# An encoder layer on one core: the order of VectorE and ScalarE at the start of the second FFN is written by hand for one block more

## The chip, the cores and the metric

One core of a Trainium2 chip runs the whole layer. The metric is the device time of one execution in microseconds (us). The engines are named as in the profile: PE (TensorE), DVE (VectorE), ACT (ScalarE), POOL (GpSimd), SP (the engine whose queue issues the DMAs).

## The reference

One post-norm encoder layer on 1024 tokens of width 1024, in float32: a first half-step FFN, attention beside a state-space scan, a second half-step FFN, and a gated embedding, each followed by a layer norm. The change lies in the second FFN:

```
gate, up = split(x @ w_in)            # w_in: 1024 x 5632, so 2816 gate and 2816 up columns
x = LN2(alpha*x + 0.5*((silu(gate) * up) @ w_out))
```

## The kernel before

**Tiling.** The 2816 hidden columns are 22 blocks of 128, called block 0 to block 21 here. For one block, gate and up together are a product of a 1024 x 256 weight with the activations of 1024 x 1024, done as a 2 x 2 product of quadrants by a Strassen-Winograd scheme with 7 products. Two of them use the gate weights as they are (quadrants B11 and B21 of the activations; `ffn_first`, L280); the other five use sums of weight quadrants and the activation operands T2, T1, T3, T4 and B22, in this order (`ffn_rest`, L367 to 392). Each of the seven is four contraction steps of 128, and each step is three matmuls, because every float32 operand is kept as a rounded high part and a low part (hi x lo, lo x hi, hi x hi; `mm3`, L115). So one product is 12 matmuls of 128 x 512.

**What surrounds a product.** A high part is a copy on ACT (`split` L108, `put_later` L247), the low part a subtraction on DVE (`lo`, L87). A product's result lies in one of four PSUM tiles `sm`; it is read out by DVE or ACT, and only then may a later product write into that tile. In `ffn_rest`: T2's is read by the sum `u2` (L378, DVE), T1's by the copy `p5` (L381, ACT), T3's by `u3` (L384, DVE), T4's by a second sum onto `u3` (L387, DVE), B22's by the sum into `sg` (L388, DVE). After it come Silu (L389, ACT), two multiplications (L390 and 391, DVE) and the stores of `h` with their sums (`left_factors`, L339 to 363). The weight sums s1 to s4 are L267 to 270, on DVE for blocks 1 to 6 and on POOL later.

**The beginning.** Blocks 0 to 4 have their first two products made early, while the activations are still being normalised. The activation operands are made for the second half of the tokens by `Sums` (L1708 to 1735): `one` to `four` are subtractions (L1705), followed by a high part on ACT and a low part on DVE; `last` makes the high and low parts of B22 (tiles `xh` and `xl`). `in_turn` issues these so that the low part of one follows the step of the next. Blocks 0 and 1 take their weights from the ring of `blk` tiles; from block 2 on the weights come through the four tiles `raw`, whose memory is that of the eight tiles `acc1`, so the first load of `raw` waits for the last reader of those: the low parts of B22. Two loads (gate and up) serve one block.

**What sets the order.** PE executes in the order of the code (`in_order(PE)` around the whole kernel). From L1779 to L1851 DVE and ACT do too (`with self.in_order(Activation, DVE)`): instructions traced in that stretch keep their order on the engine. Everything else is placed by a scheduler, which may also set instructions of its own between those of the stretch. In the kernel before, the stretch ends with `later(*sums[2:])` for block 1; the five products of block 0 (`ffn_rest` for block 0) lie behind it and the scheduler places what reads them. For blocks 2, 3 and 4 the sum of the two early products (`first_sum`, L290) is a function that `ffn_h` calls when it reaches the block; the scheduler places it.

The names in the rows: `xET2`, `xET1`, `xET3` with h or l are T2, T1, T3; in this stretch `xl<-acc` written after `xET3` is first T4 and then B22.

Of the kernel before, what the change touches and what calls it, by code (L numbers as in the profile page):

```python
# [9 lines left out]
F32 = mybir.dt.float32  # L10
F32R = mybir.dt.float32r
BF16 = mybir.dt.bfloat16
AF = mybir.ActivationFunctionType
ALU = mybir.AluOpType
# [4 lines left out]
P = 128  # L19
S = 1024  # L20
D = 1024
NT = S // P
# [14 lines left out]
class Layer:  # L37
# [332 lines left out]
    def ffn_rest(self, X, tmp, to, blocks, p1, sg, between=(), G=None):  # L370


        between = list(between)
        nc = self.nc
        V, G, A = nc.vector, G or nc.gpsimd, nc.scalar
        b2, b1, b3, b22, b4 = blocks
        u2, u3, p5 = (tmp.tile([P, 512], F32, name=name) for name in ("u2", "u3", "p5"))
        V.tensor_tensor(out=u2, in0=p1, in1=self.product(b2, X["T2"]), op=ALU.add)  # L378
        if between:
            between.pop(0)()  # L380
        A.copy(out=p5, in_=self.product(b1, X["T1"]))  # L381
        if between:
            between.pop(0)()
        V.tensor_tensor(out=u3, in0=u2, in1=self.product(b3, X["T3"]), op=ALU.add)  # L384
        G.tensor_tensor(out=u2, in0=u2, in1=p5, op=ALU.add)
        G.tensor_tensor(out=p5, in0=u3, in1=p5, op=ALU.add)
        V.tensor_tensor(out=u3, in0=u3, in1=self.product(b22, X["T4"]), op=ALU.add)  # L387
        V.tensor_tensor(out=sg[:, 512:], in0=u2, in1=self.product(b4, X["B22"]), op=ALU.add)  # L388
        A.activation(out=sg, in_=sg, func=AF.Silu)  # L389
        V.tensor_tensor(out=sg[:, :512], in0=sg[:, :512], in1=u3, op=ALU.mult)  # L390
        V.tensor_tensor(out=sg[:, 512:], in0=sg[:, 512:], in1=p5, op=ALU.mult)
        to(sg)

    def ffn_h(self, X, wi, tmp, store, pre=(), done=0, aside=None, raws=(), mixed=None, upto=0):

        nc = self.nc

        def first(f):
            g, u = raws if f == done and raws else (self.raw(wi[f, 0]), self.raw(wi[f, 1]))
            p1, sg = (pre[f]() if callable(pre[f]) else pre[f]) if f < len(pre) else self.ffn_first(X, tmp, tmp.tile([P, S], F32, name="sg"), g)
            return (g, u, tmp), p1, sg

        prev = None
        for f in range(done, NF + 1):
            s = first(f) if f < NF else None
            self.pop(2)
            if prev:  # L410
                left = mixed if f == done + 1 and mixed else self.mixed_sums(*prev[0], nc.vector if f <= upto + 1 else nc.gpsimd)

                self.ffn_rest(X, tmp, lambda h: store(f - 1, h), [b() if callable(b) else self.split(b) for b in left], *prev[1:], G=nc.vector if f == NF or f <= upto + 1 else None)
            for _ in range(0 if f < 4 or not aside else 2 if f % 4 == 0 and f > 4 else 1):
                aside.pop(0)()
            prev = s
# [1106 lines left out]
    def run(self):  # L1523
        nc, tc, I = self.nc, self.tc, self.I
# [7 lines left out]
        with ExitStack() as c:  # L1532
            pool = c.enter_context(tc.tile_pool(name="xE", bufs=1))
            tmp = self.ffn_work(c, 0)
            tmp.more()
            tmp.all()
            hS, store = self.left_factors(0, tmp)
            wpool, wT, steps = self.right_sums(c, 0, I["wo1"])
            with self.in_order(mybir.EngineType.Activation, mybir.EngineType.DVE):
                X, pre, blocks0, raws1, blocks1 = self.begin(pool, tmp, wpool)  # L1540
# [20 lines left out]
        with ExitStack() as c:  # L1561
# [4 lines left out]
            blocks0, aside = [], []  # L1566
# [112 lines left out]
        with ExitStack() as xc:  # L1679
            pool = xc.enter_context(tc.tile_pool(name="xE", bufs=1))  # L1680
            X = {n: [pool.tile([P, 4, 512], F32R, name=f"xE{n}{j}") for j in "hl"] for n in ("T1", "T2", "T3")}
            X["B11"], X["B21"], X["B22"] = self.unit(0, 0), self.unit(0, 1), self.unit(1, 0)
            V = nc.vector
            tmp = self.ffn_work(xc, 1)
            tmp.more()

            def w(i, j, to=None):
                r = self.ring.tile([P, 1024], F32, name="blk") if to is None else to
                nc.sync.dma_start(out=r, in_=I["wi2"][i, j])
                return r  # L1690
# [9 lines left out]
            def plain(t):  # L1700
                for do in [put(name, t, acc[t + i].rearrange("p (k t) -> p k t", k=4), 2) for i, name in enumerate(("B11", "B21"))]:
                    do()
# [32 lines left out]
            def in_turn(steps):  # L1735

                waiting = None
                for step in steps:
                    do = step()
                    if waiting:  # L1740
                        waiting()
                    waiting = do
                waiting()

            def gate(g):
                return zip(*[self.split_later(g[:, m]) for m in (lo, hi)])

            def later(*dos):
                for do in dos:
                    do()  # L1750
# [8 lines left out]
            blocks0 = {}  # L1759
            pre = []  # L1760
            X["T4"] = self.unit(1, 1)
            def left_block(i):
                blocks0[i], do = self.split_later(left[i])
                return do

            with self.in_order(mybir.EngineType.Activation, mybir.EngineType.DVE):
                left, sums = self.mixed_steps(g0, u0, tmp, V)
                later(*sums[:2])
                plain(0)
                later(*sums[2:])  # L1770
                plain(2)
                r5, r6, r7 = (Row(t) for t in (5, 6, 7))
                r5.half(0)
                r5.half(1)
                r5.root()
                r5.factors()
                r5.shift()

                r6.half(0)  # L1779
                r7.half(0)  # L1780
                w0, lo0 = gate(g0)
                w1, lo1 = gate(sgs[1])
                later(*lo0)
                r6.half(1)
                r6.root()
                flip(4)
                later(*lo1)
                r6.factors()
                r6.shift()
                r7.half(1)  # L1790
                r7.root()
                w2, lo2 = gate(sgs[2])
                lo_s2 = left_block(0)
                lo_a22 = left_block(3)
                s = {t: Sums(t, tmp.tile([P, 512], F32, name=n)) for t, n in ((4, "u3"), (5, "u2"))}
                s[4].one()
                t14 = s[4].put1()
                r7.factors()
                r7.shift()
                s[4].two()  # L1800
                t24 = s[4].put2()
                s[5].one()
                t15 = s[5].put1()
                s[5].two()
                t25 = s[5].put2()
                p0 = first(w0)
                later(lo_a22, t14, t15)
                pre.append(self.first_kept(sgs[0], p0))
                w3, lo3 = gate(sgs[3])
                lo_s1 = left_block(1)  # L1810
                later(*lo2, t24, t25, lo_s2)
                p1 = first(w1, lambda: flip(6))
                later(*lo3, lo_s1)
                s.update({t: Sums(t, tmp.tile([P, 512], F32, name=n)) for t, n in ((6, "h3"), (7, "p5"))})
                s[6].one()
                s[6].two()
                self.first_copy(sgs[1], p1)
                w4, lo4 = gate(sgs[4])
                t26 = s[6].put2()
                s[7].one()  # L1820
                s[7].two()
                t27 = s[7].put2()
                t26()
                t16 = s[6].put1()
                t27()
                t17 = s[7].put1()
                pre.append(self.first_sum(sgs[1], p1))

                def both(f, p):
                    for q, m in zip(p, (hi, lo)):  # L1830
                        nc.scalar.copy(out=sgs[f][:, m], in_=q)
                    pre.append(lambda: self.first_sum(sgs[f], [None, sgs[f][:, lo]]))
                both(2, first(w2))
                later(t16, t17, *lo4)
                p3 = first(w3)
                in_turn([s[t].three for t in range(4, NT)])
                both(3, p3)
                lo_s3 = left_block(2)
                both(4, first(w4))
                lo_s3()  # L1840
                in_turn([s[t].four for t in range(4, NT)])
                left_block(4)()
                g1, u1 = w(1, 0), w(1, 1)
                left, sums = self.mixed_steps(g1, u1, tmp, V)
                later(*sums[:2])
                in_turn([s[t].last for t in range(4, NT)])
                b2 = self.split(left[0])
                later(*sums[2:])
            blocks0 = [blocks0[i] for i in range(5)]
            hS, store = self.left_factors(1, tmp)  # L1850
            self.ffn_rest(X, tmp, lambda h: store(0, h), blocks0, *pre[0], G=V)  # L1851
            actx.close()
            self.open_raw(rctx, 4)
            tmp.all()
# [103 lines left out]
```

## Time and profile before

| | us |
|---|---|
| median of 3 runs | 1958.57 (1957.98 to 1959.1) |
| the profiled execution | 1959.67 |
| its span, first to last instruction | 1957.8 |
| PE busy in the span | 1931.1 (99%) |
| PE waiting in the beginning of the second FFN | 3.81 in one piece |

The profiled execution is one run on its own, 1.10 us above the median, and 1.87 us of it lie outside the span. The times in the rows count from the span's start. A row of the timeline is an instruction or a run of equal ones: start, duration, engine, line, operation, out<-in. What stands in brackets is the time for which the engine stood idle before it, and what ended the idle time.

### The profile page before, as it was taken

The page shows a single profiled execution, that of the slowest core. Times are in us where ns is not written, and L with a number is a line of the kernel's source. Part 1 is how long each engine was busy: PE and PEld are TensorE (multiplying, and loading weights), DVE is VectorE, ACT ScalarE, POOL GpSimd, SP SyncE. Part 2 cuts the span into 40 slices and gives each one's busy share as a digit, 9 for nine tenths or more (in the row PEclk, how much of TensorE's full clock was granted, in tenths as well). Part 3 has the DMA queues.
Part 4 walks back from the last instruction along what each step waited for, and adds up shares of the span by engine and source line. Part 5 has one row for each costly group of instructions (what it writes and reads, how often), then busy time and mean ns, then how long its engine had stood idle before and what let it go on. Part 6 is the DMA issues. An engine that isn't in the chain of part 4 may idle for free.

```text
span 1957.8 us, 25643 instructions
## 1 busy us (share of the span) xinstructions
PE 1931.1 (99%) x9132; PEld 1611.0 (82%) x9132; DVE 1525.2 (78%) x2364; ACT 880.5 (45%) x1509; POOL 416.2 (21%) x310
## 2 busy tenths in 40 slices
PE   8999999999999999999999999999999999999998
PEld 7888888888888889888888788788888888888886
DVE  7977777767679658759998778997687777877698
ACT  6433333334444125538887776633333334443311
POOL 0144545430001132011221001003545440001011
PEclk9999999999999999999999999999999999999999
DMA  8434554549865102231003473253545439986122
GB/s 300 137 125 155 193 178 145 194 174 381 280 228 197 55 38 68 88 121 45 5 1 109 135 270 119 84 175 138 187 154 194 153 138 338 341 267 221 37 76 97
DMA packets 147713, 310.34 MB, mean 159 GB/s; under 512 B 18128, under 2 KB 30800, under 8 KB 147584
## 3 DMA queue, kind: packets, MB, share of 16 engines
q1 hardware_dynamic: 147584, 308.69, 44.9%
q8 instruction: 72, 1.18, 0.2%
q14 instruction: 57, 0.47, 0.1%
HBM read 217.21 MB, written 91.42 MB: 158 GB/s over the span
## 4 chain that ended last, share of the span: by engine, by line
PE 94%; DVE 3%; ACT 1%; issue 1%; DMA 1%; POOL 0%; SPq 0%; DVEq 0%; ACTq 0%
PE sm L122 59%; PE big L508 12%; PE sm L508 9%; PE big L122 3%; PE big L1151 3%; PE sm L1173 2%; PE sm L1188 1%; PE sm L1189 1%; PE sm L1262 1%; DVE nm L1158 1%; DVE conv L969 1%; PE sm L1363 0%; PE sm L1273 0%; PE big L1669 0%; PE sm L224 0%
## 5 line engine op out<-in xcount | busy, mean ns | idle before, releaser
L122 PE MATMUL sm<-xh,blk 128*128 128x512 f32 x1424 | 441.9, 391 | 0.0
L122 PEld LDWEIGHTS sm<-xh,blk 128*128 128x128 f32 x1424 | 268.7, 189 | 55.6
L122 PE MATMUL sm<-xl,blk 128*128 128x512 f32 x736 | 285.3, 391 | 3.8 <-DVE xl L87 3.8
L122 PE MATMUL sm<-blk,xl 128*128 128x512 f32 (+2 forms) x784 | 238.4, 371 | 0.2 <-ACT xn_t L1002 0.2
L122 PE MATMUL sm<-blk,xh 128*128 128x512 f32 (+2 forms) x584 | 203.2, 379 | 0.3 <-DVE accr L1456 0.2
L108 ACT CAST blk<-raw 128x512 fp32r<-128x512 f32 (+1 forms) x168 | 101.2, 611 | 216.2 <-PE sm L122 130.1
L87 DVE TENSOR_TENSOR blk<-s,blk 128x512 fp32r<-128x512 f32 x176 | 150.9, 863 | 36.8 <-ACT blk L108 35.9
L87 DVE TENSOR_TENSOR blk<-raw,blk 128x512 fp32r<-128x512 f32 (+1 forms) x168 | 144.9, 866 | 37.0 <-ACT blk L108 36.4
L108 ACT CAST blk<-s 128x512 fp32r<-128x512 f32 x172 | 105.6, 622 | 145.4 <-PE sm L122 125.4
L122 PEld LDWEIGHTS sm<-xl,blk 128*128 128x128 f32 x736 | 138.8, 189 | 32.8 <-issue 4.2
L122 PEld LDWEIGHTS sm<-blk,xl 128*128 128x128 f32 x784 | 143.0, 188 | 24.0 <-ACT xn_t L1002 0.5
L178 POOL TENSOR_TENSOR ln_k<-ln_k,mhalf 128x1 f32<-128x1 f32 x32 | 36.9, 1158 | 583.1 <-DVE ln_k L177 578.2
L508 PE MATMUL big<-xh 128*128 128x512 f32 x576 | 138.8, 390 | 0.0
L267 POOL TENSOR_TENSOR s<-raw 128x512 f32<-128x512 f32 x34 | 55.0, 1617 | 389.0 <-DVE blk L87 293.3
L87 DVE TENSOR_TENSOR xh<-blk,xh 128x1024 fp32r<-128x1024 f32 x78 | 95.3, 1222 | 47.4 <-ACT xh L454 39.7
L454 ACT CAST xl<-blk 128x1024 fp32r<-128x1024 f32 x76 | 80.1, 1054 | 113.2 <-PE sm L508 41.0
L454 ACT CAST xh<-blk 128x1024 fp32r<-128x1024 f32 x78 | 82.2, 1054 | 105.9 <-PE big L508 44.2
L122 PEld LDWEIGHTS sm<-blk,xh 128*128 128x128 f32 x584 | 109.9, 188 | 20.4 <-DVE accr L1456 0.6
L508 PEld LDWEIGHTS big<-xh 128*128 128x128 f32 x576 | 107.9, 188 | 22.2
L87 DVE TENSOR_TENSOR xl<-blk,xl 128x1024 fp32r<-128x1024 f32 x76 | 92.8, 1221 | 41.9 <-ACT xl L454 34.2
L508 PE MATMUL big<-xl 128*128 128x512 f32 x480 | 115.8, 390 | 0.0
L122 PE MATMUL sm<-xET2h,blk 128*128 128x512 f32 x352 | 108.6, 390 | 0.0
(336 smaller groups left out, 4018.0 us busy)
## 6 DMA issues: line engine op xcount, KB each, us to landing
raw<-in_wi_dram SPq DMA_DIRECT2D x81, 512.0 KB
blk<-hS SPq DMA_DIRECT2D x154, 256.0 KB
hS<-h SPq DMA_DIRECT2D x88, 256.0 KB
wr<-in_wo_dram SPq DMA_DIRECT2D x44, 512.0 KB
blk<-wT SPq DMA_DIRECT2D x88, 256.0 KB
hS<-sg SPq DMA_DIRECT2D x66, 256.0 KB
wT<-wr SPq DMA_DIRECT2D x66, 256.0 KB
blk<-in_wo_dram SPq DMA_DIRECT2D x66, 256.0 KB
```

What stands on the lines that cost most here:

```text
L87: (eng or self.nc.vector).tensor_tensor(out=out, in0=full, in1=hi.bitcast(F32), op=ALU.subtract)
L108: self.nc.scalar.copy(out=b[:, 0, :n], in_=src)
L122: self.nc.tensor.matmul(ps, lhsT=a, rhs=b, start=(i == 0), stop=(i == n - 1))
L178: nc.gpsimd.tensor_tensor(out=r, in0=v, in1=self.mhalf[:, :1], op=ALU.pow)
L267: lambda: G.tensor_tensor(out=s1, in0=a21, in1=a22, op=ALU.add),
L454: A.copy(out=b[:, :, 0], in_=r)
L508: nc.tensor.matmul(ps[q], lhsT=b[:, 0, x, cut], rhs=b[:, 1, y], start=j == i == 0, stop=j == NP - 1 and i == 2)
L969: nc.vector.scalar_tensor_tensor(out=a[:, o], in0=ps[:, o.start + d - c:o.stop + d - c], scalar=cw[:, j, tap:tap + 1], in1=a[:, o], op0=AL ...
L1151: nc.tensor.matmul(ps[:, n * 512:(n + 1) * 512], lhsT=Q[:, h, q0:q0 + P], rhs=K[:, h // 4, j, n * 512:(n + 1) * 512], start=j == 0, stop=j ...
L1158: nc.vector.tensor_reduce(out=nm, in_=ps, axis=AX.X, op=ALU.max, negate=True)
L1173: nc.tensor.transpose(out=pt[:, k], in_=pr[:, kk * P:(kk + 1) * P], identity=self.ident)
L1188: nc.tensor.matmul(po, lhsT=vw, rhs=pth[k // 4][:, k % 4], start=k == 0, stop=False)
```

## The change

The hand-written order is carried on to the end of block 0. The five products of block 0 are issued inside the stretch, and the instructions that read them are written between those that were there: `u2` directly after the low part of block 0's last weight block, then the high and low parts of B22, then the first two weight sums of block 1, `p5`, `u3`, the low part of block 1's first weight block, and so on. What is left of `ffn_rest` for block 0 is a function `ffn_end`. The call of `first_sum` for blocks 2 to 4 is put behind the last DVE instruction traced so far.

```diff
-        A.activation(out=sg, in_=sg, func=AF.Silu)
+        self.ffn_end(sg, u3, p5, to)
+
+    def ffn_end(self, sg, u3, p5, to):
+        V = self.nc.vector
+        self.nc.scalar.activation(out=sg, in_=sg, func=AF.Silu)
...
-            p1, sg = (pre[f]() if callable(pre[f]) else pre[f]) if f < len(pre) else self.ffn_first(X, tmp, tmp.tile([P, S], F32, name="sg"), g)
+            if f < len(pre) and callable(pre[f]):
+                with self.behind(mybir.EngineType.DVE):
+                    p1, sg = pre[f]()
+            else:
+                p1, sg = pre[f] if f < len(pre) else self.ffn_first(X, tmp, tmp.tile([P, S], F32, name="sg"), g)
...
                 in_turn([s[t].four for t in range(4, NT)])
+                p1, sg = pre[0]
+                q = self.product(blocks0[0], X["T2"])
                 left_block(4)()
+                u2, u3, p5 = (tmp.tile([P, 512], F32, name=name) for name in ("u2", "u3", "p5"))
+                V.tensor_tensor(out=u2, in0=p1, in1=q, op=ALU.add)
+                in_turn([s[t].last for t in range(4, NT)])
                 g1, u1 = w(1, 0), w(1, 1)
                 left, sums = self.mixed_steps(g1, u1, tmp, V)
                 later(*sums[:2])
-                in_turn([s[t].last for t in range(4, NT)])
+                nc.scalar.copy(out=p5, in_=self.product(blocks0[1], X["T1"]))
+                V.tensor_tensor(out=u3, in0=u2, in1=self.product(blocks0[2], X["T3"]), op=ALU.add)
                 b2 = self.split(left[0])
+                V.tensor_tensor(out=u2, in0=u2, in1=p5, op=ALU.add)
+                V.tensor_tensor(out=p5, in0=u3, in1=p5, op=ALU.add)
                 later(*sums[2:])
-            blocks0 = [blocks0[i] for i in range(5)]
+                V.tensor_tensor(out=u3, in0=u3, in1=self.product(blocks0[3], X["T4"]), op=ALU.add)
+                V.tensor_tensor(out=sg[:, 512:], in0=u2, in1=self.product(blocks0[4], X["B22"]), op=ALU.add)
             hS, store = self.left_factors(1, tmp)
-            self.ffn_rest(X, tmp, lambda h: store(0, h), blocks0, *pre[0], G=V)
+            self.ffn_end(sg, u3, p5, lambda h: store(0, h))
```

No instruction is added or taken away on any engine, and PE's order is the same. Three places show what moves. The lines of the changed kernel are up to 17 higher than those of before.

**Place 1.** DVE around the low parts of B22 (`xl_11092`; `xl_11142` is T4). Before:

```order
L87 TENSOR_TENSOR xl_11142<-acc_10237,xh_11141 128x4x128 x2
L87 TENSOR_TENSOR blk<-s_11146,blk 128x512
L384 TENSOR_TENSOR u_11606<-u_11605,sm 128x512
L385 TENSOR_TENSOR u_11605<-u_11605,p_11607 128x512
L267 TENSOR_TENSOR s_11575<-blk 128x512
L386 TENSOR_TENSOR p_11607<-u_11606,p_11607 128x512
L268 TENSOR_TENSOR s_11576<-s_11575,blk 128x512
L87 TENSOR_TENSOR xl_11092<-acc_10423,xh_11091 128x4x128 x2
L87 TENSOR_TENSOR xl_11092<-acc_10601,xh_11091 128x4x128 x2
L387 TENSOR_TENSOR u_11606<-u_11606,sm 128x512
```

The same place now (L1854 is the sum `u2`, L1860 the sum `u3`, L1862 and L1863 the sums with `p5`):

```order
L87 TENSOR_TENSOR xl_11142<-acc_10237,xh_11141 128x4x128 x2
L87 TENSOR_TENSOR blk<-s_11146,blk 128x512
L1854 TENSOR_TENSOR u_11584<-sg,sm 128x512
L87 TENSOR_TENSOR xl_11092<-acc_10423,xh_11091 128x4x128 x2
L87 TENSOR_TENSOR xl_11092<-acc_10601,xh_11091 128x4x128 x2
L267 TENSOR_TENSOR s_11600<-blk 128x512
L268 TENSOR_TENSOR s_11601<-s_11600,blk 128x512
L1860 TENSOR_TENSOR u_11585<-u_11584,sm 128x512
L87 TENSOR_TENSOR blk<-s_11601,blk 128x512
L1862 TENSOR_TENSOR u_11584<-u_11584,p_11586 128x512
L87 TENSOR_TENSOR blk<-s_11600,blk 128x512
```

`u3`, the two sums with `p5` and two weight sums stood ahead of the low parts of B22 and stand behind them now; `u2` stood ahead of T4's first low part and stands directly ahead of B22's.

**Place 2.** DVE where the first weight sum of block 2 (`s_11819<-raw`, it needs the first loads of `raw`) stands. Before:

```order
L387 TENSOR_TENSOR u_11606<-u_11606,sm 128x512
L87 TENSOR_TENSOR blk<-s_11576,blk 128x512
L269 TENSOR_TENSOR s_11577<-blk 128x512
L270 TENSOR_TENSOR s_11578<-blk,s_11576 128x512
L87 TENSOR_TENSOR blk<-s_11575,blk 128x512
L87 TENSOR_TENSOR blk<-s_11577,blk 128x512
L87 TENSOR_TENSOR blk<-blk 128x512
L87 TENSOR_TENSOR blk<-s_11578,blk 128x512
L267 TENSOR_TENSOR s_11819<-raw 128x512
```

Now (L1865 reads T4's product of block 0, L1866 B22's):

```order
L1863 TENSOR_TENSOR p_11586<-u_11585,p_11586 128x512
L269 TENSOR_TENSOR s_11602<-blk 128x512
L270 TENSOR_TENSOR s_11603<-blk,s_11601 128x512
L267 TENSOR_TENSOR s_11819<-raw 128x512
L1865 TENSOR_TENSOR u_11585<-u_11585,sm 128x512
L1866 TENSOR_TENSOR sg<-u_11584,sm 128x512
L87 TENSOR_TENSOR blk<-s_11602,blk 128x512
L87 TENSOR_TENSOR blk<-blk 128x512
```

The sum that needs the loads stood behind all low parts of block 1's weights; now the reading of two products and three of those low parts stand behind it.

**Place 3.** DVE in block 2, where T4's product is read (`u_11843<-u_11843,sm`) and with it a PSUM tile is given back, which T4's product of block 3 writes in the changed program. Before:

```order
L386 TENSOR_TENSOR p_11844<-u_11843,p_11844 128x512
L352 TENSOR_TENSOR h_11811<-sg,h_11807 128x512
L267 TENSOR_TENSOR s_12233<-raw 128x512
L388 TENSOR_TENSOR sg<-u_11842,sm 128x512
L387 TENSOR_TENSOR u_11843<-u_11843,sm 128x512
L87 TENSOR_TENSOR blk<-s_12087,blk 128x512
```

Now:

```order
L388 TENSOR_TENSOR sg<-u_11842,sm 128x512
L87 TENSOR_TENSOR blk<-s_12086,blk 128x512
L87 TENSOR_TENSOR blk<-s_12085,blk 128x512
L352 TENSOR_TENSOR h_11811<-sg,h_11807 128x512
L290 TENSOR_TENSOR sg<-sg 128x512
L87 TENSOR_TENSOR blk<-s_12087,blk 128x512
L87 TENSOR_TENSOR blk<-raw,blk 128x512
L387 TENSOR_TENSOR u_11843<-u_11843,sm 128x512
```

The reading of T4's product moves three low parts of weights and one `first_sum` (L290) further back. The three `first_sum` of blocks 2, 3 and 4, which stood between T3's and T4's low parts before, stand further back now, two of them between place 2 and the last row of place 3.

## Rows read from the trace of the kernel before

**Rows 1.** The page: the span, and busy time by engine.

```profile
span 1957.8 us, 25643 instructions
...
PE 1931.1 (99%) x9132; PEld 1611.0 (82%) x9132; DVE 1525.2 (78%) x2364; ACT 880.5 (45%) x1509; POOL 416.2 (21%) x310
```

**Rows 2.** Waits of PE: waited for, us in total, times, longest.

```profile
PE sm L122 <- DVE blk L87: 6.9, 1, 6.9
PE sm L1262 <- DVE state L1279: 4.4, 3, 1.9
PE sm L122 <- DVE xl L87: 3.8, 1, 3.8
```

**Rows 3.** Timeline of PE: first matmuls of products in blocks 0, 1.

```profile
1246.02 0.39 PE L122 MATMUL sm<-xET2l,blk 128*128 128x512 f32 x1
...
1248.74 0.39 PE L122 MATMUL sm<-xET1l,blk 128*128 128x512 f32 x1
...
1254.18 0.39 PE L122 MATMUL sm<-xl,blk 128*128 128x512 f32 x1
...
1260.86 0.76 PE L122 MATMUL sm<-xl,blk 128*128 128x512 f32 x1 [3.81 <-DVE xl L87]
...
1269.21 0.39 PE L122 MATMUL sm<-xET1l,blk 128*128 128x512 f32 x1
```

**Rows 4.** Stretches: length, busy by engine (instructions), PE's granted clock, DMA share, GB/s.

```profile
1246.00:1257.00 11.00, 11.00 (x49) 8.83 (x47) 9.26 (x15) 6.37 (x12) 0.00 (x0) 1.00 0.00 1
...
1260.86:1266.60 5.74, 5.74 (x14) 4.49 (x15) 4.67 (x8) 2.94 (x4) 0.00 (x0) 0.50 0.82 295
...
1280.00:1293.00 13.00, 13.00 (x59) 10.76 (x58) 13.00 (x23) 4.56 (x8) 0.00 (x0) 1.00 0.52 179
```

**Rows 5.** The same columns, beside another wait of PE (1.95 us).

```profile
1096.00:1097.00 1.00, 0.00 (x0) 0.00 (x0) 1.00 (x3) 1.00 (x5) 0.00 (x0) 1.00 0.65 252
1097.00:1098.00 1.00, 0.66 (x3) 0.64 (x4) 1.00 (x3) 1.00 (x2) 0.00 (x0) 1.00 0.54 205
```

**Rows 6.** Timeline of DVE ahead of the wait.

```profile
1240.54 0.69 DVE L290 TENSOR_TENSOR sg<-sg 128x512 f32<-128x512 f32 x1
...
1248.94 0.69 DVE L378 TENSOR_TENSOR u<-sg,sm 128x512 f32<-128x512 f32 x1 [0.55 <-PE sm L122]
1249.54 0.69 DVE L87 TENSOR_TENSOR xl<-acc,xh 128x512 fp32r<-128x512 f32 x1
...
1253.34 0.69 DVE L87 TENSOR_TENSOR blk<-s,blk 128x512 fp32r<-128x512 f32 x1
...
1258.23 2.49 DVE L87 TENSOR_TENSOR xl<-acc,xh 128x512 fp32r<-128x512 f32 x4
```

**Rows 7.** Timeline of ACT ahead of the wait.

```profile
1245.67 1.14 ACT L1831 COPY sg<-sm 128x512 f32<-128x512 f32 x2
1247.22 1.23 ACT L247 CAST xh<-acc 128x512 fp32r<-128x512 f32 x2 [0.41 <-DVE acc L1705]
...
1253.12 2.17 ACT L247 CAST xh<-acc 128x512 fp32r<-128x512 f32 x4
```

**Rows 8.** SP's first loads of `raw`, and DVE at their landing.

```profile
1260.78 9.54 SPq L94 DMA_DIRECT2D raw<-in_wi_dram  x5
...
1266.74 0.69 DVE L267 TENSOR_TENSOR s<-raw 128x512 f32<-128x512 f32 x1 [1.21 <-issue]
...
1267.95 0.68 DVE L388 TENSOR_TENSOR sg<-u,sm 128x512 f32<-128x512 f32 x1
```

**Rows 9.** Timeline of DVE in blocks 2 and 3.

```profile
1283.11 0.69 DVE L267 TENSOR_TENSOR s<-raw 128x512 f32<-128x512 f32 x1
...
1294.54 0.69 DVE L388 TENSOR_TENSOR sg<-u,sm 128x512 f32<-128x512 f32 x1
1295.13 0.69 DVE L387 TENSOR_TENSOR u<-u,sm 128x512 f32<-128x512 f32 x1
...
1302.05 0.69 DVE L384 TENSOR_TENSOR u<-u,sm 128x512 f32<-128x512 f32 x1 [0.81 <-PE sm L122]
```

## Prediction

> **What bounds the kernel now.** The page comes first: PE is busy for 1931.1 of 1957.8 us [rows 1], so only its idle time can be won, and next to that what PE does slowly. The list of PE's waits is read second: in all of the span three pieces are over a microsecond in total, and the one of 3.8 us in a single piece, behind a low part that DVE writes to a tile `xl`, is the one in the stretch of the change [rows 2]. The timeline of PE says where it is: block 0's last product, the one with B22, starts at 1260.86 after 3.81 us of idle time, behind the low parts of B22 [rows 3, 6]. The stretches say what follows: before the wait the granted clock is 1.00 (2.4 GHz); in the 5.74 us from the first matmul behind it, it is 0.50 (1.2 GHz), and by 1280 it is back at 1.00 [rows 4]. Elsewhere a wait of 1.95 us (at 1097) left the clock at 1.00 [rows 5]. From 1266.6 to the tail PE has no wait, so a gain here stays to the end unless a new wait takes it.
>
> **What the wait costs.** The ruler is a product at full clock: T2's of block 0 starts at 1246.02, T1's at 1248.74, so 2.72 us. T4's of block 0 starts at 1254.18 and T1's of block 1 at 1269.21: three products (T4, B22, and T2 of block 1) in 15.03 us [rows 3]. At 2.72 each they are 8.16. The place costs 15.03 - 8.16 = 6.87 us: 3.81 idle and 3.06 for the slow matmuls behind it.
> "TensorE: Matmul & The Clock Gate" of the Trainium skill (section Terms) prices time at a lowered clock at that time multiplied by the share of pulses held back; an estimate from it is 5.74 x 0.5 = 2.87 us, and the sum by it would be 6.68 instead of 6.87. I keep the rows' 6.87, since it comes from two starts at full clock, one on either side.
>
> **Place 1: when B22 is ready.** PE would start B22's product at 1254.18 + 2.72 = 1256.90. From above: if nothing ahead of `u2` comes any earlier, the low part of block 0's last weights starts at 1253.34 as before [rows 6]; then `u2` at 1253.94 and the four low parts from 1254.54, one each 0.60 (the step between DVE's instructions, from 1248.94 to 1249.54 in [rows 6]). They end by 1257.1, and PE waits 0.2 us. ACT's four high parts ended at 1255.29 before [rows 7] and don't come later. So even the worst case takes away nearly all.
> From below: T4's first low part stood behind `u2`, which waited for T2's product until 1248.94 [rows 6]. Now it waits only for its high part on ACT, which follows ACT's copies ending at 1246.81 [rows 7]: with 0.62 for the cast it starts near 1247.5 instead of 1249.54. The three `first_sum` that go from ahead of it (the first at 1240.54 [rows 6]) make sure that DVE is there. T4's low parts and their subtractions took from 1249.54 to 1253.34, so block 0's last low part starts at 1251.3, `u2` at 1251.9, B22's from 1252.5 to 1255.0. That is 1.9 us ahead of PE. I take this value; PE's wait goes, and without it nothing on the rows is left that would lower the clock: -6.87 us.
>
> **Place 1 and 2: what is late next.** The instructions put behind B22 are needed too. DVE is free at 1254.9; after the two weight sums and `u3`, block 1's first low part is the fourth: 1254.9 + 3 x 0.60 + 0.69 = 1257.4, against T2 of block 1 on PE at 1256.90 + 2.72 = 1259.62. Nine instructions end at 1260.3. Then the first weight sum of block 2 waits for the loads of `raw`. Before, SP issued the loads at 1260.78, straight after B22's last low part, and the sum started at 1266.74 after 1.21 us of idle time, so 5.96 from issue to use [rows 8]. Now the loads go at 1255.05 and the sum can start at 1261.0, some 0.6 us of idle time for DVE. Behind it stand the reading of T4's and B22's products and the low part of s3: that ends at 1261.0 + 3 x 0.60 + 0.69 = 1263.5, and T3 of block 1 needs it at 1265.06 (1259.62 + 2 x 2.72). Spare: 1.6 us.
>
> **Place 3: the backlog of DVE.** PE comes 6.87 us earlier to blocks 2 and 3, where DVE is busy for 13.00 of 13.00 us [rows 4]. From 1283.11 to 1294.54 it starts 19 instructions after the first, 0.6016 each [rows 9]. In the changed order 55 instructions run from block 2's first weight sum to the reading of T4's product of block 2, two of the postponed `first_sum` (1.2 us) among them. The last starts at 1261.0 + 54 x 0.602 = 1293.5 and ends at 1294.2. T4's product of block 3 needs its PSUM tile at 1254.18 + 15 x 2.72 = 1294.98. Spare: 0.8 us, the smallest in the stretch. If DVE stood there as late as before (1295.13 + 0.69 = 1295.8 [rows 9]), PE would wait 0.9. With block 4 PE gets seven products per block instead of five, and before DVE stood idle again from 1301 (0.81 us, waiting for PE [rows 9]); so the backlog ends there. The other edits cost nothing: ACT's instructions are the same, and it is busy for 6.37 of 11.00 and 4.56 of 13.00 us [rows 4]; were that cover gone, a cast would cost PE at most its 0.62.
>
> **The sum.** 1959.67 of the profiled execution less 6.87 is 1952.8. The median is 1.10 below that execution: 1958.57 - 6.87 = 1951.7.
>
> **The rivals.**
> A. DVE's backlog turns into a new wait at block 3 (or at T3 of block 2). For it: the spare of 0.8 us rests on 54 steps; a step longer by 0.02 makes 1.1 us. Against it: the step is the same over 19 instructions in the rows. Price: 1 to 2.5 us of idle time, too short to lower the clock by [rows 5]. The time is 1952.7 to 1954.2, in the middle 1953.4.
> B. The clock falls for another reason than the wait, or doesn't come back with it. Then only the idle time goes: 1958.57 - 3.81 = 1954.8. For it: the rows show one case alone. Against it: the clock was 1.00 up to the wait and 0.50 directly behind it [rows 4].
> C. The loads of `raw` land late, and this costs more than the wait removed. DVE's sum of block 2 stands now ahead of the reading of T4's product and of s3's low part, so every microsecond past 1262.6 (1261.0 and the spare 1.6) is one in which PE waits before T3 of block 1. That DVE goes on in order behind a waiting instruction is in the rows: the reading of B22's product at 1267.95 stood behind the sum waiting for the load [rows 8].
> The spec table of the same page of the Trainium skill says that VectorE's queue is strictly first in, first out; the trace agrees by that row, and by this rule nothing can pass the sum.
> Where the loads land as late as before, at 1266.74, PE idles 1266.74 - 1262.6 = 4.1 us, the clock falls as it did behind 3.81, 3.06 more, and the time is 1958.57 - 6.87 + 7.2 = 1958.9. The point at which it becomes slower than before is an idle time of 3.81, a landing at 1266.4; a landing two microseconds later than before gives 1960.9, and it takes one past 1270.3 to be slower by over 0.2%. Against it: the loads wait for the last reader of their memory, which is still B22's last low part, and the DMA engines moved nothing from 1246 to 1257 [rows 4].
>
> **How the numbers follow.** Forecast 74%, A 14%, B 4%, C 8% (half of it within 0.2% of before, half slower by more). What a measurement can tell here is 0.2%, 3.9 us: faster means under 1954.65, slower over 1962.49. Faster: the forecast, and A nearly whole: 0.86. Same: the end of A, B, and half of C: 0.10. Slower: 0.04. The forecast's own range is the worst case of place 1 (+0.2) and the spread of the runs shown (1957.98 to 1959.1, so about 0.6 to either side): 1951.1 to 1952.5. To hold 8 of 10 it takes in A and stops short of B and C: 1950.6 to 1954.4.
>
> **What would show it.** In the changed profile the row of PE waiting for `xl` is gone, or under 0.3 us; B22's product starts 2.72 after T4's; the stretch behind it has the clock at 1.00; T1 of block 1 starts 8.16 after T4 of block 0. B22's low parts end 1.5 us or more before that product. The loads of `raw` are issued about 5.7 us earlier and the first weight sum of block 2 starts at about 1261. At block 3's T4 PE waits less than 0.5. It would be wrong if a new wait of PE over 1 us stands in blocks 1 to 4, if the clock is at 0.50 there, or if PE's later products don't all start some 6.9 us earlier.

## The result, and the profile after

The changed kernel takes 1953.14 us (median of 9 runs, 1952.0 to 1954.15) against 1958.57 (9 runs beside it, 1957.25 to 1960.25): a ratio of 0.9972 with a 95% interval of 0.9964 to 0.998, so 5.43 us less, 3.9 to 7.1 by the interval. The profiled execution takes 1952.0 and its span is 1950.2; the spans of the two profiled executions, before and after, differ by 7.6.

The list of PE's waits in the changed kernel: waited for, us in total, times, longest.

```profile
PE sm L122 <- DVE blk L87: 6.9, 1, 6.9
PE sm L1270 <- DVE state L1287: 2.5, 2, 1.6
PE sm L1270 <- ACT xs L1264: 1.7, 1, 1.7
PE sm L1270 <- DVE state L1284: 0.8, 1, 0.8
```

The row on `xl` of [rows 2] is gone. From 1240 to the end no wait is listed. What is left lies ahead of that and was there before as well (the 1.7 put down to ACT is one of three waits in the same place that [rows 2] puts down to DVE, 4.4 together).

The timeline of PE in the changed kernel: first matmuls of T4 and B22 of block 0, T2 and T1 of block 1, and T4 of block 3.

```profile
1253.48 0.39 PE L122 MATMUL sm<-xl,blk 128*128 128x512 f32 x1
...
1256.20 0.39 PE L122 MATMUL sm<-xl,blk 128*128 128x512 f32 x1
...
1258.92 0.39 PE L122 MATMUL sm<-xET2l,blk 128*128 128x512 f32 x1
...
1261.64 0.39 PE L122 MATMUL sm<-xET1l,blk 128*128 128x512 f32 x1
...
1294.28 0.39 PE L122 MATMUL sm<-xl,blk 128*128 128x512 f32 x1
```

Each of these four products starts 2.72 after the one ahead of it, and from T4 of block 0 to T1 of block 1 (called T4 to T1 below) it is 8.16 where [rows 3] had 15.03.

The stretches of the changed kernel: length, busy time of PE, PEld, DVE, ACT, POOL, PE's granted clock, DMA share, GB/s.

```profile
1246.00:1257.00 11.00, 11.00 (x50) 9.13 (x49) 10.70 (x18) 6.71 (x13) 0.00 (x0) 1.00 0.17 57
1257.00:1266.60 9.60, 9.60 (x44) 7.95 (x43) 9.60 (x17) 6.33 (x10) 0.00 (x0) 1.00 0.41 155
...
1280.00:1293.00 13.00, 13.00 (x59) 10.78 (x58) 13.00 (x23) 4.82 (x9) 0.00 (x0) 1.00 0.56 183
```

The stretch that had the clock at 0.50 [rows 4] has it at 1.00, and PE is busy throughout.

The timeline of DVE and of SP's queue in the changed kernel: B22's low parts, the first weight sum of block 2, the low part of s3, the reading of T4's product of block 2; then the first loads of `raw`.

```profile
1251.66 2.49 DVE L87 TENSOR_TENSOR xl<-acc,xh 128x512 fp32r<-128x512 f32 x4
...
1259.79 0.68 DVE L267 TENSOR_TENSOR s<-raw 128x512 f32<-128x512 f32 x1
...
1261.59 0.68 DVE L87 TENSOR_TENSOR blk<-s,blk 128x512 fp32r<-128x512 f32 x1
...
1292.27 0.68 DVE L387 TENSOR_TENSOR u<-u,sm 128x512 f32<-128x512 f32 x1
```

```profile
1254.18 1.75 SPq L94 DMA_DIRECT2D raw<-in_wi_dram  x4
```

B22's low parts end at 1254.15, 2.05 ahead of its product; before, they ended at 1260.72, when PE had stood idle for 3.67 [rows 3, 6]. The loads go at 1254.18, and the sum that needs them starts 5.61 later with no idle time of DVE in front of it, where [rows 8] had 1.21. T4's product of block 2 is read by 1292.95, 1.33 ahead of the product that needs its tile.

### The profile page after: what moved, and what is told of

Read it like the earlier page. It is cut to its first block, busy times and chain, and to the rows that moved or that the text cites. A ratio compares the mean times of both kernels' runs of the same rounds, so it can differ in the third digit from the quotient of the medians.

```text
span 1950.2 us, 25647 instructions
## 1 busy us (share of the span) xinstructions
PE 1927.4 (99%) x9132; PEld 1607.7 (82%) x9132; DVE 1526.2 (78%) x2364; ACT 880.9 (45%) x1509; POOL 416.0 (21%) x310
## 4 chain that ended last, share of the span: by engine, by line
PE 95%; DVE 3%; ACT 1%; issue 0%; DMA 0%; POOL 0%; DVEq 0%; SPq 0%; ACTq 0%
PE sm L122 59%; PE big L516 12%; PE sm L516 9%; PE big L122 3%; PE big L1159 3%; PE sm L1181 2%; PE sm L1196 1%; PE sm L1197 1%; PE sm L1270 1%; PE sm L1371 1%; DVE nm L1166 1%; DVE conv L977 1%; PE sm L1281 0%; PE big L1677 0%; PE big L224 0%
```

## Experiments

The mechanism was clear from these rows; the size was not: 6.87 forecast, 5.43 measured. Two theories stood. P: the wait costs 6.87 in every execution, and the runs scatter. V: the cost differs between executions, and the one that the prediction read was a dear one.

### The same two kernels once more

No edit. The kernel before three times more, the changed kernel once.

> The kernel before once more, unchanged. Theory P (the prediction): the wait costs 6.87 us in every execution, 3.81 idle and 3.06 by the slow clock. Another profiled execution then shows T4 of block 0 to T1 of block 1 in 15.0 (14.9 to 15.1), the idle piece 3.8, the clock 0.50 behind it, and the ratio to before is 1.000 (0.999 to 1.001). Theory V: the slow part differs between executions and the one that was read was a costly one; then the same distance is shorter here, 13.6 to 14.6, with the idle piece still 3.8.

> The kernel before a third time, for one more profiled execution. The two so far took 15.03 and 13.84 from T4 of block 0 to T1 of block 1, with the same idle piece (3.81 and 3.80). Theory V (the slow part differs from execution to execution and 3.06 was a costly one): idle 3.8, the distance between 13.0 and 15.1, and the mean slow part of all looks near 5.4 - 3.8 = 1.6 to 1.9, which the medians ask for. Theory P (3.06 is the rule, 1.88 the exception): 15.0.

> The kernel before a fourth time. Three looks: 15.03, 13.84 and 13.76 from T4 of block 0 to T1 of block 1, so a slow part of 3.06, 1.88 and 1.79 beside the idle piece of 3.8. Theory V: again 3.8 idle, and a slow part of 1.6 to 1.9 in most executions, so 13.6 to 13.9 here. If 15.0 comes again, the costly kind is not rare, and the medians' 5.4 must come from somewhere else too.

> The changed kernel once more, unchanged. Theory P: T4 of block 0 to T1 of block 1 takes 8.16 again, no wait over 0.5 us in blocks 0 to 4, and the time is 1958.57 - 6.87 = 1951.7, ratio 0.9965 (0.9960 to 0.9970); the first comparison's 5.4 to 5.7 was scatter of the runs. Theory V: the gain in most executions is 5.4 to 5.7 and the ratio settles at 0.9971 to 0.9973.

Measured: the kernel before 1958.33, ratio to itself 0.9999 (0.9990 to 1.0008); single runs 1957.43 and 1958.96; the changed kernel 1953.10 against 1958.51, 0.9972 (0.9961 to 0.9983). The timelines of PE say where the executions differ. In the first repeat: T4 of block 0, B22 behind the wait, T1 of block 1.

```profile
1254.90 0.39 PE L122 MATMUL sm<-xl,blk 128*128 128x512 f32 x1
...
1261.59 0.47 PE L122 MATMUL sm<-xl,blk 128*128 128x512 f32 x1 [3.80 <-DVE xl L87]
...
1268.74 0.39 PE L122 MATMUL sm<-xET1l,blk 128*128 128x512 f32 x1
```

The stretches of that execution, with the columns as above:

```profile
1257.40:1261.50 4.10, 0.39 (x2) 0.00 (x0) 4.10 (x8) 1.14 (x2) 0.00 (x0) 1.00 0.00 0
1261.60:1262.00 0.40, 0.40 (x2) 0.36 (x3) 0.40 (x2) 0.00 (x0) 0.00 (x0) 1.00 0.00 0
1262.00:1263.00 1.00, 1.00 (x5) 0.76 (x4) 1.00 (x3) 0.00 (x0) 0.00 (x0) 0.57 0.61 131
1263.00:1264.00 1.00, 1.00 (x4) 0.81 (x3) 1.00 (x3) 0.72 (x2) 0.00 (x0) 0.50 0.93 332
1264.00:1265.00 1.00, 1.00 (x4) 0.81 (x3) 1.00 (x3) 0.98 (x3) 0.00 (x0) 0.50 0.96 373
1265.00:1266.00 1.00, 1.00 (x4) 0.73 (x4) 1.00 (x3) 1.00 (x1) 0.00 (x0) 0.73 0.68 246
```

The idle piece is the same, 3.80. But PE began again with the granted clock at 1.00 (2.4 GHz), the clock fell to 0.50 (1.2 GHz) only then, and it was back within the microsecond from 1265. In [rows 4] it was at 0.50 from the first matmul behind the wait. The second repeat, the same three products, and its clock at the first of them and at its return:

```profile
1253.31 0.39 PE L122 MATMUL sm<-xl,blk 128*128 128x512 f32 x1
...
1259.98 0.76 PE L122 MATMUL sm<-xl,blk 128*128 128x512 f32 x1 [3.80 <-DVE xl L87]
...
1267.07 0.39 PE L122 MATMUL sm<-xET1l,blk 128*128 128x512 f32 x1
```

```profile
1260.00:1261.00 1.00, 1.00 (x3) 0.81 (x4) 1.00 (x3) 0.00 (x0) 0.00 (x0) 0.50 0.13 20
...
1263.00:1264.00 1.00, 1.00 (x5) 0.78 (x5) 1.00 (x3) 0.98 (x2) 0.00 (x0) 0.87 1.07 426
```

The return of the clock in the execution that the prediction read:

```profile
1266.00:1267.00 1.00, 1.00 (x4) 0.77 (x4) 0.26 (x1) 0.00 (x0) 0.00 (x0) 0.59 1.02 414
```

All profiled executions together, from the same rows of each; the cost is T4 to T1 less 8.16, and the slow part is the cost less the idle piece:

| execution | T2 of block 0 starts | T4 to T1 | cost | slow part | T1 of block 1 to the span's end |
|---|---|---|---|---|---|
| before, the one the prediction read | 1246.02 | 15.03 | 6.87 | 3.06 | 688.6 |
| before, first repeat | 1246.74 | 13.84 | 5.68 | 1.88 | 688.6 |
| before, second repeat | 1245.14 | 13.76 | 5.60 | 1.80 | 688.6 |
| before, third repeat | 1246.51 | 13.82 | 5.66 | 1.86 | 688.6 |
| changed | 1245.32 | 8.16 | 0 | 0 | 688.6 |
| changed, repeat | 1245.02 | 8.17 | 0 | 0 | 688.6 |

What follows: V. From T1 of block 1 on, no two of these executions differ by 0.1 us. They differ ahead of the stretch (1.7 us between the earliest and the latest) and in the slow part. Three of four have a cost of 5.6 to 5.7, near the 5.4 by which the medians differ. The profiled pair's 7.6 is 6.87 and 0.70 of the start.

What made the one dear is not that its clock fell early: the second repeat too had the clock at 0.50 from its first matmul, and it is the cheapest. It is how long PE worked at 0.50: by the granted clock of each microsecond, 6.0 us in the execution that the prediction read (the stretch of 5.74 in [rows 4] ends before the clock's return), and 3.4, 3.3 and 3.4 us in the repeats. Half of each is 3.0, 1.7, 1.6 and 1.7, the slow part but for 0.1 to 0.2. Why the clock stayed down longer in that one execution is not shown by any run.

### PE kept busy while it waits

Into the kernel before, ahead of B22's product of block 0, go matmuls that fill the wait; DVE's order stays. There are runs with 16, 12 and 8 of them; this is the edit for 16:

```diff
     def product(self, w, x, fill=0):
         ps = self.pss()
+        for i in range(fill):
+            self.nc.tensor.matmul(ps, lhsT=self.fill_w[:, 0, :P], rhs=self.fill_x[:, i % 4], start=True, stop=True)
...
+            self.fill_w, self.fill_x = blocks0[3], X["T4"][0]
-            self.ffn_rest(X, tmp, lambda h: store(0, h), blocks0, *pre[0], G=V)
+            self.ffn_rest(X, tmp, lambda h: store(0, h), blocks0, *pre[0], G=V, fill=16)
```

> The kernel before with 16 matmuls more on PE, ahead of B22's product of block 0, into the same PSUM tile, which the product then writes from its start; they need nothing that is late. At 0.227 each (2.72 / 12) they fill 3.63 of the 3.81 us for which PE waited, and the low parts of B22 come no earlier. Theory P: the clock fell because PE stood idle, so with PE busy it stays at 1.00, only 0.2 us of waiting is left, T4 of block 0 to T1 of block 1 takes 15.03 - 3.06 = 11.97, and the time is 1958.57 - 3.06 = 1955.5, ratio 0.9984. Theory V in numbers: 1956.7 to 1957, ratio 0.9991. Rival B of the prediction (the clock falls for another reason): 1958.6, ratio 1.000, and 0.50 in the stretch behind the wait.

> The kernel before with 8 filling matmuls instead of 16 ahead of B22's product: they take 1.81 of the 3.81 us, so one idle piece of 2.0 is left, and B22's low parts come no earlier. Theory I (how long PE stands idle in one piece decides whether the clock falls; 1.95 at 1097 left it at 1.00): the clock stays at 1.00, T4 of block 0 to T1 of block 1 takes 8.16 + 3.81 + 0.3 = 12.3 as with 16, and the time is that of 16 matmuls, 1956.4, ratio 0.9991. Rival (any idle piece of this size lowers it at times): the distance is 13 to 15, the time 1958.5, ratio 1.000.

> The kernel with 8 filling matmuls once more. Its eleven times fell into two groups, five from 1956.10 to 1956.88 with a mean clock of 0.999, six from 1957.82 to 1958.50 with 0.998; the profiled one was of the first, with the clock at 1.00 throughout. Theory V (the clock falls in some executions and not in others, and that is the difference): an execution of the second group shows the same idle piece of 2.0, a stretch at 0.50 behind it, and T4 of block 0 to T1 of block 1 in 12.2 + 1.7 = 13.9; one of the first group shows 12.2 again. Rival: a time of the second group with 12.2 here, the difference being elsewhere.

> The kernel before with 12 filling matmuls: 2.72 of the 3.81 us are filled and an idle piece of 1.1 is left. With 16 (0.18 left) ten of eleven runs had the mean clock 0.999, with 8 (2.0 left) five of eleven, with 0 (3.8 left) none. Theory I (the longer PE stands idle, the likelier the clock falls): eight or more of the runs at 0.999, the median near that of 16 matmuls, 1956.4 to 1957.0, and T4 of block 0 to T1 of block 1 in 12.2. Rival: the fall has nothing to do with the length, and half of the runs show it, as with 8.

PE with 16 filling matmuls (L254), then the stretches at the end of the wait:

```profile
1254.11 0.39 PE L122 MATMUL sm<-xl,blk 128*128 128x512 f32 x1
...
1256.83 3.79 PE L254 MATMUL sm<-xh,blk 128*128 128x512 f32 x16
1260.80 0.47 PE L122 MATMUL sm<-xl,blk 128*128 128x512 f32 x1 [0.18 <-DVE xl L87]
1261.10 0.63 PE L122 MATMUL sm<-xh,blk 128*128 128x512 f32 x2
...
1263.64 0.39 PE L122 MATMUL sm<-xET2l,blk 128*128 128x512 f32 x1
...
1266.36 0.39 PE L122 MATMUL sm<-xET1l,blk 128*128 128x512 f32 x1
```

```profile
1260.00:1261.00 1.00, 0.82 (x4) 0.42 (x3) 1.00 (x3) 0.00 (x0) 0.00 (x0) 1.00 0.00 0
1261.00:1262.00 1.00, 1.00 (x5) 0.81 (x5) 1.00 (x3) 0.00 (x0) 0.00 (x0) 1.00 0.32 86
```

PE with 8, at the end of the wait:

```profile
1260.13 0.47 PE L122 MATMUL sm<-xl,blk 128*128 128x512 f32 x1 [1.98 <-DVE xl L87]
```

| filling | idle left | T4 to T1, profiled | median | ratio (interval) | runs by mean clock 0.999, 0.998 |
|---|---|---|---|---|---|
| 16 | 0.18 | 12.25 | 1956.41 | 0.9991 (0.9982 to 0.9999) | 10, 1 |
| 12 | 1.08 | 12.24 | 1956.78 | 0.9990 (0.9981 to 0.9999) | 10, 1 |
| 8 | 1.98, 1.99 | 12.21, 12.24 | 1957.82 | 0.9993 (0.9984 to 1.0003) | 5, 6 |
| none (first repeat) | 3.80 | 13.84 | 1958.33 | 0.9999 (0.9990 to 1.0008) | 0, 11 (six of them 0.997) |

What follows: with no operand any earlier, a kernel whose PE is kept busy is 2.10 us faster (1958.51 - 1956.41), and in its profiled execution the clock stays at 1.00. So the slow part belongs to the idle time, and rival B is out. It is 1.6 to 2.1 in size (13.84 - 12.25 by the traces, 2.10 by the medians); P had expected 3.06. With 8, the times of eleven runs lie in two groups, 1956.10 to 1956.88 with the higher mean clock and 1957.82 to 1958.50 with the lower, some 1.7 apart: an idle piece of 2.0 seems to lower the clock in about half of the executions. That is not shown. It is read from times and mean clocks alone, and the mean clock counts more than this place: in the repeat of the changed kernel it is 0.998 with the clock at 1.00 in the whole stretch, because it falls at the end of the span, behind PE's last matmul (0.50 from 1944 to 1949), where it costs nothing. Both profiled executions with 8 were of the first group (the second one, a single run, took 1956.68), so the fall itself wasn't seen there.

### B22's low parts later in the changed kernel

```diff
-                in_turn([s[t].last for t in range(4, NT)])
                 g1, u1 = w(1, 0), w(1, 1)
...
                 V.tensor_tensor(out=p5, in0=u3, in1=p5, op=ALU.add)
+                in_turn([s[t].last for t in range(4, NT)])
                 later(*sums[2:])
```

> The changed kernel with B22's high and low parts written later: behind the first weight sums of block 1, u3, the first low part and the two sums with p5. u3 waits for T3's product (1253.5 in the changed kernel), four more instructions follow, so B22's low parts start at 1256.0 and end at 1258.5: PE idles 2.4 before B22's product. The loads of raw wait for the same low parts and go 4.4 later than in the changed kernel, the first sum of block 2 starts near 1264.2 and DVE runs behind from there: a second wait of PE, 1.5 to 2.0, before T3's product of block 2, which waits for DVE to give back a PSUM tile. This is rival C of the prediction in small. Theory I: neither piece lowers the clock; 4.2 of idle time and nothing else, 1953.1 + 4.2 = 1957.3, ratio 0.9994. Rival: the clock falls behind the 2.4 at times, 1.9 more, 1959.2, ratio 1.0003. If late loads cost nothing, 2.4 alone: 1955.5.

Measured: 1956.91 against 1958.62, 0.9991 (0.9982 to 1.0000). PE at the wait and at T1 of block 1; T4 of block 0 starts at 1252.93:

```profile
1258.21 0.50 PE L122 MATMUL sm<-xl,blk 128*128 128x512 f32 x1 [2.40 <-DVE xl L87]
...
1265.39 0.39 PE L122 MATMUL sm<-xET1l,blk 128*128 128x512 f32 x1
```

The stretches behind it:

```profile
1259.00:1260.00 1.00, 1.00 (x5) 0.74 (x4) 1.00 (x3) 1.00 (x3) 0.00 (x0) 0.69 0.78 188
1260.00:1261.00 1.00, 1.00 (x4) 0.81 (x3) 1.00 (x2) 0.45 (x1) 0.00 (x0) 0.50 1.02 381
```

The first wait is the 2.40 that the order gave. Theory I fell: behind 2.40 the clock is at 0.50 in this execution, and T4 to T1 is 12.46, a cost of 4.30 with a slow part of 1.90. The second wait did not come: the loads, issued at 1258.18, had landed when DVE started their sum at 1263.12, 4.94 later and not 5.6, and PE's slow part gave DVE 1.9 more; together that is more than the 1.8 that was expected. The total came out near the expectation (1957.3) by luck, with two errors of opposite sign: 1.8 of wait that was missing, and 1.9 of slow clock that was not counted. Rival C, a sum waiting for late loads ahead of block 1's readings, was not tried as such: here that sum stands behind them.

### One part alone, and all but one part

The kernel before with B22's parts moved ahead of the two weight sums, nothing else:

```diff
                 left_block(4)()
+                in_turn([s[t].last for t in range(4, NT)])
                 g1, u1 = w(1, 0), w(1, 1)
                 left, sums = self.mixed_steps(g1, u1, tmp, V)
                 later(*sums[:2])
-                in_turn([s[t].last for t in range(4, NT)])
```

> The kernel before with one edit: B22's high and low parts are written ahead of the first two weight sums of block 1; block 0's five products and their readers stay with the scheduler. In this order u3 still stands ahead of the low parts (it waits for T3's product, 1254.38 in the kernel before), so they end near 1257.5 instead of 1260.72: PE idles 0.6 before B22's product. The reading of B22's product now stands ahead of the low part of block 1's first weights, which so ends near 1261.8 while PE wants it at 1260.3: a second wait of 1.4 before T2 of block 1. Theory P: two short waits, 2.0 together, leave the clock at 1.00; T4 of block 0 to T1 of block 1 takes 8.16 + 2.0 = 10.2, and the time is 1958.57 - 6.87 + 2.0 = 1953.7, ratio 0.9975. Rival: the edit alone is the whole change, no wait is left, 1951.7. Rival: waits close together lower the clock as the one wait did, 3.06 more, 1956.8.

Measured: 1954.88, 0.9982 (0.9973 to 0.9991), 3.63 less than before. PE at B22 of block 0 and T2 of block 1:

```profile
1257.22 0.50 PE L122 MATMUL sm<-xl,blk 128*128 128x512 f32 x1 [0.47 <-DVE xl L87]
1257.56 0.63 PE L122 MATMUL sm<-xh,blk 128*128 128x512 f32 x2
...
1260.29 0.50 PE L122 MATMUL sm<-xET2l,blk 128*128 128x512 f32 x1
1261.64 0.73 PE L122 MATMUL sm<-xET2h,blk 128*128 128x512 f32 x2 [0.85 <-DVE blk L87]
```

The two short waits stand where the order put them (0.6 and 1.4 expected), the clock is at 1.00 in all of the stretch, and T4 to T1 is 10.40, 2.24 more than at full clock without a wait. The 1953.7 expected was 1.2 too low: it was worked out with the 6.87; with the repeats' cost it is 1958.51 - 5.65 + 2.24 = 1955.1. One edit brings about two thirds of the gain; the scheduler, left to place the readers of block 0, puts the reading of B22's product ahead of a low part for which PE waits next.

The changed kernel with `first_sum` left to the scheduler again:

```diff
-            if f < len(pre) and callable(pre[f]):
-                with self.behind(mybir.EngineType.DVE):
-                    p1, sg = pre[f]()
-            else:
-                p1, sg = pre[f] if f < len(pre) else self.ffn_first(...)
+            p1, sg = (pre[f]() if callable(pre[f]) else pre[f]) if f < len(pre) else self.ffn_first(...)
```

> The changed kernel without the last part of the change: the three first_sum of blocks 2 to 4 go where the scheduler puts them, ahead of T4's low parts. Theory P: 1.8 us of DVE work stand again ahead of B22's low parts, but DVE waited there for 0.8 anyway, so they end 0.2 to 1.0 ahead of B22's product instead of 2.05 ahead, PE doesn't wait, place 3 gets 0.2 to 1.2 more room, and the time is that of the changed kernel, ratio 0.9972. Rival: this part carries the gain; then PE waits 0.2 or more for xl, or DVE is late at block 3, and the ratio is 0.998 or more.

Measured: 1953.13, 0.9972 (0.9962 to 0.9982). DVE's low parts of B22 in it:

```profile
1253.61 2.49 DVE L87 TENSOR_TENSOR xl<-acc,xh 128x512 fp32r<-128x512 f32 x4
```

They end at 1256.10, 1.11 ahead of the product (1257.21): the postponed sums brought 0.94 of spare and no time. Place 3 has 1.62 of spare in this kernel, 0.29 more than in the changed one. The worst case of place 1 (0.2 of wait) didn't come even so, since T4's first low part no longer stands behind `u2`.

### More work for DVE in its full stretch

```diff
-    def mixed_sums(self, g, u, tmp, G):
+    def mixed_sums(self, g, u, tmp, G, extra=0):
...
-        for do in steps:
+        for do in steps + [steps[3]] * extra:
             do()
...
-self.mixed_sums(*prev[0], nc.vector if f <= upto + 1 else nc.gpsimd)
+self.mixed_sums(*prev[0], nc.vector if f <= upto + 1 else nc.gpsimd, 5 if upto == 5 and f == done + 2 else 0)
```

> The changed kernel with one weight sum of block 2, s4, written five times more with the same operands: 3.0 us of work more for DVE, which is busy for 13.00 of 13.00 us there. The scheduler spreads the five over blocks 1 and 2, so the low part of s4 is late: it is the 38th instruction from the first weight sum of block 2 (1259.79) and ends at 1259.79 + 37 x 0.602 + 0.69 = 1282.8, B22's product of block 2 needs it at 1283.6. The reading of T4's product of block 2 is now the 52nd and ends at 1291.2, three instructions earlier than in the changed kernel. Theory P (place 3 is a question of order, and DVE's full stretch still has room): no wait over 0.3 us in blocks 1 to 4, 1953.1, ratio to before 0.9972. Rival A of the prediction (the backlog is at its limit; 3.0 of work against 1.3 of spare): 1.7 us of waiting in block 2 or 3, 1954.8, ratio 0.9981.

Measured: 1952.74 against 1958.72, 0.9973 (0.9963 to 0.9983), and no wait of PE in blocks 0 to 4. On DVE, the low part of s4 of block 2 and the reading of T4's product of block 2; on PE, the second matmul of the product that needs the first, and the product of block 3 that needs the tile of the second:

```profile
1283.22 0.68 DVE L87 TENSOR_TENSOR blk<-s,blk 128x512 fp32r<-128x512 f32 x1
...
1291.65 0.68 DVE L387 TENSOR_TENSOR u<-u,sm 128x512 f32<-128x512 f32 x1
```

```profile
1284.16 0.61 PE L122 MATMUL sm<-xh,blk 128*128 128x512 f32 x2
...
1294.82 0.39 PE L122 MATMUL sm<-xl,blk 128*128 128x512 f32 x1
```

The low part is done 0.26 before it is wanted. 3.0 us of added work cost nothing, so "13.00 of 13.00 busy" did not mean that the room was used up. But the scheduler made another order of it: T4's product of block 2 is read 2.49 ahead of its need, where the changed kernel has 1.33. So rival A's place had more room here, not less, and what a later reading would cost is not shown.

## Why the prediction was right, and where its size was off

- **What bounds the kernel, and that a gain stays to the end.** Right. The distance from T1 of block 1 to the end is 688.6 in six executions of two kernels.
- **What the wait costs.** The idle term, 3.81, measured 3.80 in each of three repeats. The mis-sized term is the slow part: 3.06 forecast, 1.80 to 1.88 in the three repeats. The step that failed is "I keep the rows' 6.87, since it comes from two starts at full clock": the ruler of 2.72 a product was good, but it was laid on one execution. With the repeats' mean cost of 5.65 the sum is 1958.57 - 5.65 = 1952.9; 1953.14 and 1953.10 were measured. The step to the median took over the same error: it subtracted 6.87 from a median whose runs, by three profiled executions of four, hold 5.65. That the execution stood 1.10 above the median didn't show this by itself, since the repeats at 1959.11 and 1958.96 have the short slow part and a later start.
- "TensorE: Matmul & The Clock Gate" of the Trainium skill (section Part 1: The HAM clock gate) says that the same kernel shows a different count of slow matmuls from run to run. The traces of the kernel before agree (slow parts of 1.80 to 3.06), and it speaks against taking one execution for the rule. The price in its section Terms, which the prediction names, held: by the granted clock, microsecond by microsecond from 1262 to 1266, the first repeat lost 0.43 + 0.50 + 0.50 + 0.27 = 1.70 of its 1.88. The rest is about the size of a gap in the count: the idle piece runs from the end that the profile gives the last matmul ahead of it, 0.17 after the next product would have started (1254.90 + 2.72 = 1257.62 against 1261.59 - 3.80 = 1257.79).
- **Place 1.** Right. Low parts 1.9 ahead of PE forecast, 2.05 measured.
- **Place 2.** Right in its conclusion, a little dear. 5.96 from issue to use was taken for the loads' landing and gave 0.6 of idle time; the sum started 5.61 after the issue without waiting. The low part of s3 ended 2.1 ahead of T3 of block 1 instead of 1.6.
- **Place 3.** Right. 0.8 forecast, 1.33 measured; the 0.5 between them is the idle time at the loads that did not come. The step of 0.602 between DVE's instructions held over all 54. The wait of 0.9 given for a DVE as late as before is 0.8 by its own numbers (1295.82 - 1294.98); nothing else hangs on it.
- **The rivals.** A: no new wait; its price was not tested, since the 3.0 us more work came with an order that gave its place more room. B: out by the filling matmuls. C: the loads were not late. A's remark that 1 to 2.5 us of idle time are too short to lower the clock went beyond the 1.95 of [rows 5] and is wrong: 2.40 lowered it in the profiled execution with B22's low parts written later.

The range held the time by luck as far as the size goes: its upper part was there for rival A, which did not come. The likeliest case's own range (1951.1 to 1952.5) did not hold it, for want of a spread of the slow part.

## What to carry to other kernels

A wait that lowers PE's clock has a part that every execution pays (the idle time) and a part that differs between executions; read the second from several profiles before it goes into a sum, and find the point behind the place from which all executions take the same time. Which wait is the next one is seen by writing down the order that the scheduler makes of a single edit: moving only the late operand brought two thirds of the gain here. A full engine is no bound as such: what counts is the spare of each instruction that PE waits for.

## What the runs showed of the hardware that was not expected

- After an idle piece of 3.8 us, PE's clock fell before PE began again in two profiled executions (0.50 in the stretch from the first matmul) and after it had begun in two (in the first repeat 1.00, then 0.50 in the stretch from 1263). That did not set the cost, which was 3.06 and 1.80 in the first two, 1.88 and 1.86 in the others; PE's time at 0.50 did (6.0 us, and 3.3 to 3.4 us). Why an execution is of one kind or the other stays open.
- PE starts again slowly even with the clock at 1.00: with 16 filling matmuls, B22's product behind 0.18 of idle time took 2.84 (1260.80 to 1263.64) instead of 2.72, its first matmul 0.30 instead of 0.227; behind 0.47 the first one took 0.34.
